# One layer with delta-rule heads, latent attention and experts: the output norm of a head pair apart from its scan, and another order of the opening

## The chip, the cores and the metric

The kernel runs on one core of a Trainium2 chip. Its time is the time of one execution on the device in microseconds (us); several executions are timed and the median is given. A profiled execution is a further one, with its own time.

## The reference

A stream `x` of 512 tokens and a context `ctx` of 256 tokens, 1024 channels each, go through one layer. What matters here is its first half:

```python
mod = silu(cond) @ ada_w + ada_b            # six vectors: shift, scale, gate, twice
h   = rms_norm(x) * g * (1 + scale) + shift # x by c, ctx by c_ctx
p   = h @ w_in                              # q, k, v, z of 8 heads, alpha, beta, and more
q, k, v = silu(short_conv(...))             # five taps over the tokens
o   = gated_delta_chunked(...)              # per head, forwards and backwards: ctx first
y   = rms_norm(o, dn_norm_g) * silu(z)      # the output norm of a head
```

After that come latent attention over the 768 tokens, the merge of both branches, and sixteen experts with 320 slots in all by expert choice.

## The kernel before, in words

**Layout.** Tokens stand in tiles of 128. `XT` holds the normed tokens transposed, eight tiles of 128 channels by 768 tokens (512 of `x`, then 256 of `ctx`). `HT` holds the modulated `x`, `HC` the modulated `ctx`; each value and each weight is split into a high and a low part, and a product is three matmuls (`begin`, and `mm3` at L140 to L142): high by high, high by low, low by high. The low part of a weight is `raw - high`.

**The opening, 0 to some 75 us.** `modulate(i)`, i = 0 to 3, makes 256 channels of the modulation. `aq{i}` (2 MB of `ada_w`, in two halves) is loaded, TensorE multiplies it (`pa{i}`), ScalarE copies the product (`ms{i}`), TensorE turns it into columns (`pc{i}`), VectorE makes shift and scale (`md`, `gs1`), ScalarE writes the high part of two tiles of `HT` (`ht`) and of `HC` (`hc`), and the low part is a product (`hm`) and a subtraction. `begin(i, name)` starts the projection of the first head's k, q and v (`wf0`, `wf1`, `wf2`) and of the second head's k (`wf3`) over those two tiles, six matmuls for each. `tokens(k)` and `tokens_ctx(k)` transpose one tile of channels of `x` and of `ctx`. All of it is written in one fixed order: `TE`, `SE`, `VE` and `GP` are wrappers (`_Pinned`) that keep each engine's instructions in the order of the program. All the large loads are issued on SyncE's queue, one after the other; an issue that waits for its buffer holds up the ones behind it.

**The head pairs, 75 to some 700 us.** For four pairs p of heads: `head_k`, `head_q`, `head_v`, `head_z` project, convolve and norm (`load_split` makes the low part `wl_*` of a weight on VectorE, L338); `prepare(p)` makes the decay matrices (TensorE `GH`, `gr`, ScalarE `D` with a Relu and an exponential, L759 and L760, VectorE `W` and `A`); `inverse(p)` inverts them, a long loop on VectorE; `scan(p)` walks over six steps of tokens in both directions. At its end `scan` norms the pair's output `O`: eight squares with a row sum on ScalarE (L996), four small operations on GpSimd (L997 to L1000), a product on VectorE (L1001), then eight transposes `py` on TensorE (L1009) and a product with the gate `Z`.

**The order of the pairs.** Each of these is a generator that `_Emit` steps: a job has a rank, a list of jobs that must be done before it (`after`), and each `yield` gives a cost and a latency on a planned clock. The job of lowest rank that is ready is written next, and the framework's scheduler orders what follows from that. `scan(p)` waits for `inverse(p)`, `prepare(p)` for the heads of p and for `dn[p - 1]`, which is the scan before, its norm and its `py` included; the heads of pair p wait for `dn[p - 2]`. Between the pairs stand jobs that fill TensorE: the projections for the gates (`gt`, `wl_gt`) and the latent attention, and `ada(q)`, the other modulation vectors (loads `aw`, matmuls `pa` at L168 and L170).

Of the kernel before, what the change touches and what calls it, by code (L numbers as in the profile page):

```python
# [20 lines left out]
P = 128  # L21
# [153 lines left out]
def hybrid_block(ctx: ExitStack, tc: tile.TileContext, I, out, dbg=None):  # L175
# [79 lines left out]
    for t in range(6):  # L255
        xt = vw.tile([P, D], F32, name=f"xt{t}")
        src = I["x"][0, t * P:(t + 1) * P, :] if t < 4 else I["ctx"][0, (t - 4) * P:(t - 3) * P, :]
        nc.sync.dma_start(xt, src)
        xn.append(xt)
# [112 lines left out]
    def split_first(j):  # L372
# [7 lines left out]
        first[nm] = (w, pdn([P, 512], f"pl_{nm}"))  # L380
# [30 lines left out]
    def modulate(i):  # L411
# [6 lines left out]
        m = vw.tile([P, 512], F32, tag="ms", name=f"ms{i}", bufs=2)  # L418
        SE.activation(m, pa, AF.Copy)
        yield  # L420
        pc = ptr([P, 4, P], f"pc{i}")
        for k in range(4):
            TE.transpose(pc[:, k], m[:, k * P:(k + 1) * P], ident)
# [8 lines left out]
        yield  # L432
        for sl, j in SEG:
            if j:
                yield
            for kk in range(2):
                k, h = 2 * i + kk, (HC if j else HT)[i][:, kk]
                if j == 0:
                    ys[kk] = vw.tile([P, TOK], F32, tag=f"xt{kk}", name=f"hm{k}")
                y = ys[kk]  # L440
                SE.activation(h[:, 0], XT[:, k, sl], AF.Identity, bias=md[:, i, 0, kk, j:j + 1],
                              scale=gs1[:, i, kk, j:j + 1])
                VE.tensor_scalar(y[:, sl], XT[:, k, sl], gs1[:, i, kk, j:j + 1], md[:, i, 0, kk, j:j + 1],
                                 op0=OP.mult, op1=OP.add)
                (GP if j else VE).tensor_sub(h[:, 1], y[:, sl], h[:, 0].bitcast(F32))
        yield

    ys = {}

    def begin(i, *names):  # L450
        for nm in names:
            w, pl = first[nm]
# [18 lines left out]
    m = [modulate(i) for i in range(NB)]  # L471
# [3 lines left out]
    tokens(0)  # L475
    norm(4)
    tokens(1)
    norm(5)
    for k in range(2, KT):
        tokens(k)  # L480
    for k in range(2):
        tokens_ctx(k)
    next(m[0])
    split_first(0)
    next(m[0])
    next(m[0])
    split_first(1)
    split_first(2)
    next(m[1])
    next(m[1])  # L490
    begin(0, "k0", "q0")
    next(m[1])
    begin(0, "v0")
    begin(1, "k0", "q0", "v0")
    for k in range(2, KT):
        tokens_ctx(k)
    next(m[0])
    split_first(3)
    next(m[2])
    next(m[2])  # L500
    begin(0, "k1")
    next(m[2])
    next(m[1])
    begin(2, "k0", "q0")
    next(m[3])
    begin(2, "v0")
    next(m[3])
    begin(1, "k1")
    next(m[3])
    next(m[2])  # L510
# [401 lines left out]
    def scan(p, zjobs):  # L912
# [9 lines left out]
        for s in range(6):  # L922
# [68 lines left out]
            yield 0.9, 0.5, None  # L991
        tap(f"O{p}", O)
# [21 lines left out]
    seq, A_jobs, zj, dn, dp_, dd = [], {}, {}, {}, {}, {}  # L1014
# [53 lines left out]
    dn[3] = em.add(3, scan(3, zj[3]), after=[dp_[3], dn[2]])  # L1068
# [744 lines left out]
```

## Time and profile before

| | |
|---|---|
| Median of 3 runs | 1776.95 us (1773.66 to 1779.38) |
| The profiled execution | 1781.53 us, its span 1779.8 us |
| TensorE (PE) busy | 1597.0 us, 90% of the span |
| VectorE (DVE) busy | 877.9 us, 49% |
| ScalarE (ACT) busy | 593.2 us, 33% |
| GpSimd (POOL) busy | 249.8 us, 14% |
| Mean granted clock of TensorE | 0.956 of full speed |

PE is the matrix engine, PEld its loading of weights, SPq SyncE's queue of DMA issues. A row of a timeline has the start, the duration, the engine, the line, the operation, the output and its inputs, and in brackets how long the engine was idle before it and what ended that. A granted clock of 1.00 is 2.4 GHz, of 0.50 it is 1.2 GHz.

### The profile page before, as it was taken

To read this page: it belongs to the slowest core of one execution; us is meant where nothing else is said; L and a number is where in the kernel's file an instruction comes from. 1 tells how busy PE (TensorE), PEld (TensorE's weight loads), DVE (VectorE), ACT (ScalarE), POOL (GpSimd) and SP (SyncE) were. 2 spreads that over 40 slices of the span, in tenths; PEclk is the share of its full clock that TensorE was granted. 3 is DMA by queue.
4 is the path that set the end of the run, shared out by engine and by line. 5 is a ranking of instruction groups with operands and counts; after the bars stand their busy time and mean duration, and the time that the engine had idled before them with its cause. 6 is when DMAs were issued, how large, how long until landed. Compare 5 with 4: busy or idle time off the path is not lost.

```text
span 1779.8 us, 25305 instructions
## 1 busy us (share of the span) xinstructions
PE 1597.0 (90%) x9990; PEld 1102.4 (62%) x9990; DVE 877.9 (49%) x1957; ACT 593.2 (33%) x1336; POOL 249.8 (14%) x326
## 2 busy tenths in 40 slices
PE   5897999898799997889989996999999999999887
PEld 4686887786678786767777775544454444444333
DVE  3687857965787854666873436121212121213122
ACT  4576338326634334556663423100010000000000
POOL 2222021121121122323121432000000000000000
PEclk8998999999899989899989997999999999999999
DMA  9211311343122342121126965799999999999997
GB/s 309 59 48 48 90 43 48 85 159 103 48 72 76 91 132 81 53 85 42 35 67 204 288 209 203 272 413 413 413 397 413 413 413 412 414 414 413 414 413 290
DMA packets 168409, 382.31 MB, mean 215 GB/s; under 512 B 10373, under 2 KB 91491, under 8 KB 168291
## 3 DMA queue, kind: packets, MB, share of 16 engines
q1 hardware_dynamic: 163328, 372.98, 56.6%
q10 hardware_dynamic: 4963, 7.72, 1.3%
q8 instruction: 78, 1.28, 0.3%
q14 instruction: 40, 0.33, 0.1%
HBM read 366.51 MB, written 14.16 MB: 214 GB/s over the span
## 4 chain that ended last, share of the span: by engine, by line
PE 40%; DMA 9%; DVE 5%; ACT 2%; issue 2%; POOL 2%; SPq 0%; DVEq 0%; ACTq 0%; POOLq 0%
PE pd L1765 7%; PE pg L1724 6%; PE pu L1724 5%; DMA wd<-in_w_down_dram 4%; PE pg L1725 3%; PE pu L1725 3%; PE pc L1781 2%; DMA w_up<-in_w_up_dram 1%; PE pxe L1667 1%; DMA woraw<-in_w_o_dram 1%; PE pxe L1668 1%; PE pPT L1311 1%; DMA raw_ukv<-in_w_ukv_dram 1%; PE px L140 1%; PE px L142 1%
## 5 line engine op out<-in xcount | busy, mean ns | idle before, releaser
L1724 PE MATMUL pg<-w_gate,XE 128*64 128x320 f32 x496 | 178.6, 511 | 0.0
L1724 PE MATMUL pu<-w_up,XE 128*64 128x320 f32 x480 | 160.0, 487 | 3.9 <-DMA w_up<-in_w_up_dram 3.9
L1745 DVE TENSOR_TENSOR hd<-hd,pu 128x320 f32<-128x320 f32 (+1 forms) x48 | 18.6, 416 | 287.7 <-PE pu L1725 270.5
L1725 PE MATMUL pg<-w_gate,XE 128*64 128x320 f32 x496 | 157.1, 455 | 0.0
L1765 PE MATMUL pd<-wd,hd 128*64 128x512 f32 x668 | 150.6, 597 | 3.1 <-DMA wd<-in_w_down_dram 3.1
L1725 PE MATMUL pu<-w_up,XE 128*64 128x320 f32 x480 | 153.3, 444 | 0.0
L1770 ACT ACTIVATE yo<-hd 128x512 fp32r<-128x512 f32 x16 | 10.1, 629 | 344.0 <-DVE hd L1769 344.0
L1724 PEld LDWEIGHTS pu<-w_up,XE 128*64 128x64 f32 x480 | 64.6, 137 | 74.3 <-issue 38.1
L1765 PEld LDWEIGHTS pd<-wd,hd 128*64 128x64 f32 x668 | 45.0, 136 | 86.4 <-issue 76.7
L1724 PEld LDWEIGHTS pg<-w_gate,XE 128*64 128x64 f32 x496 | 66.7, 141 | 45.7 <-issue 26.0
L1725 PEld LDWEIGHTS pg<-w_gate,XE 128*64 128x64 f32 x496 | 60.4, 140 | 23.7 <-issue 10.2
L1743 ACT ACTIVATE hd<-pg 128x320 f32<-128x320 f32 (+1 forms) x48 | 16.5, 378 | 171.5 <-PE pg L1725 171.5
L1781 PE MATMUL pc<-yo 64*128 64x512 f32 x256 | 47.3, 455 | 26.1 <-ACT yo L1770 22.7
L1781 PEld LDWEIGHTS pc<-yo 64*128 64x128 f32 x256 | 23.2, 194 | 66.7 <-ACT yo L1770 35.9
L1785 DVE TENSOR_TENSOR xm<-xm,pc 128x512 f32<-128x512 f32 x72 | 45.9, 683 | 32.0 <-PE pc L1781 32.0
L1769 DVE SCALAR_TENSOR_TENSOR hd<-pd,gs,m 128x512 f32<-128x512 f32 x16 | 12.0, 751 | 97.6 <-PE pd L1765 97.6
L142 PE MATMUL pl_gt<-ht,wl_gt 128*128 128x512 f32 x128 | 51.5, 402 | 3.1 <-DVE wl_gt L338 3.1
L1671 ACT ACTIVATE XE<-pxe,mod,gs 128x256 f32<-128x256 f32 x32 | 16.3, 560 | 112.6 <-PE pxe L1668 99.9
L140 PE MATMUL pl_gt<-ht,wh_gt 128*128 128x512 f32 x128 | 53.2, 416 | 0.0
L1725 PEld LDWEIGHTS pu<-w_up,XE 128*64 128x64 f32 x480 | 49.8, 135 | 2.8
L141 PE MATMUL pl_gt<-ht,wh_gt 128*128 128x512 f32 x128 | 51.3, 400 | 0.0
L1160 DVE TENSOR_TENSOR PT<-pPT,PT 128x512 fp32r<-128x512 f32 x48 | 33.0, 688 | 24.9 <-ACT PT L1159 24.7
(623 smaller groups left out, 4214.8 us busy)
## 6 DMA issues: line engine op xcount, KB each, us to landing
w_gate<-in_w_gate_dram SPq DMA_DIRECT2D x60, 1408.0 KB, 14.9
w_up<-in_w_up_dram SPq DMA_DIRECT2D x60, 1408.0 KB, 19.8
wd<-in_w_down_dram SPq DMA_DIRECT2D x45, 1536.0 KB
aw<-in_ada_w_dram SPq DMA_DIRECT2D x32, 512.0 KB, 5.7
wd<-in_w_down_dram SPq DMA_DIRECT2D x15, 1024.0 KB, 15.9
aq<-in_ada_w_dram SPq DMA_DIRECT2D x8, 1024.0 KB, 9.2
raw_gt<-in_w_in_dram SPq DMA_DIRECT2D x16, 512.0 KB, 3.8
ring_w<-in_w_up_dram SPq DMA_DIRECT2D x3, 1408.0 KB, 12.6
```

Of the source, the lines that this page charges most:

```text
L140: nc.tensor.matmul(out, wh, xh, start=first, stop=False)
L141: nc.tensor.matmul(out, wh, xl, start=False, stop=False)
L142: nc.tensor.matmul(out, wl, xh, start=False, stop=last)
L1160: nc.vector.tensor_sub(lo, src, hi.bitcast(F32))
L1311: nc.tensor.transpose(p_[:, t * P:(t + 1) * P], Pm[:, t, kt_ * P:(kt_ + 1) * P], ident)
L1667: nc.tensor.matmul(px[:, j], X2[:, t, 0, ks], oh, start=(t == 0), stop=False)
L1724: nc.tensor.matmul(dst[c][0:64, :n], x_, w[kk][:, o:o + n], start=(k == ko[0]), stop=(k == ko[3] + 1))
L1725: nc.tensor.matmul(dst[c][64:128, :320], x_, w[kk][:, FA + c * 320:FA + c * 320 + 320], start=(k == ko[0]), stop=(k == ko[3] + 1))
L1745: nc.vector.tensor_mul(hd[pr, o:o + b - a], hd[pr, o:o + b - a], pu[c][pr, a:b])
L1765: nc.tensor.matmul(pd[64 * dh:64 * dh + 64], l_, w[:, j, dh * 512:(dh + 1) * 512], start=(i == 0), stop=(i == 10))
L1781: nc.tensor.matmul(pcs[dh], o_[ps_, t, :], y_[ps_, l, :], start=(i + l == 0), stop=(i + l == len(ys_)))
L1785: nc.vector.tensor_add(xm[t][:, sl], xm[t][:, sl], pcs[dh])
```

## The change

It has three parts.

1. **Loads and order of the opening.** The two loads of `ctx` come after the weights of the modulation and of the first heads; they go into a buffer of the tag `aq`. The first half of `aq0`, then `k0`, then its second half come first. `modulate(i)` is taken apart into `ada_block(i)`, `columns(i)` and `modulate(i, j)`, j = 0 for `x` and 1 for `ctx`; all `modulate(i, 1)` stand at the end.
2. **Engines.** The four low parts of `wf` (128 by 1024) and the eight low parts of `HC` (128 by 256) are subtracted on VectorE and not on GpSimd.
3. **The norm apart.** `scan(p)` ends with its last step (`sc[p]`), and `finish(p)` (`dn[p]`, rank p + 0.5) holds the norm and `py`. Heads of pair p wait for `sc[p - 2]`, `prepare(p)` for `sc[p - 1]`; `scan(p)` waits for `dn[p - 1]`.

```diff
-    for t in range(6):
+    for t in range(4):
         xt = vw.tile([P, D], F32, name=f"xt{t}")
-        src = I["x"][0, t * P:(t + 1) * P, :] if t < 4 else I["ctx"][0, (t - 4) * P:(t - 3) * P, :]
...
+    def load_ctx():
+        a = vr.tile([P, 2, KT, 2 * P], F32, tag="aq", name="xctx", bufs=3).rearrange("p l k c -> p (l k c)")
+        for t in range(2):
+            xn.append(a[:, t * D:(t + 1) * D])
+            nc.sync.dma_start(xn[4 + t], I["ctx"][0, t * P:(t + 1) * P, :])
...
-        GP.tensor_sub(w[1], raws[j], w[0].bitcast(F32))
...
+    def split_lo(j):
+        w = first[FIRST[j][0]][0]
+        VE.tensor_sub(w[1], raws[j], w[0].bitcast(F32))
...
-                (GP if j else VE).tensor_sub(h[:, 1], y[:, sl], h[:, 0].bitcast(F32))
...
+    def modulate(i, j):
+        sl = SEG[j][0]
+        for kk in range(2):
...
+            VE.tensor_scalar(y, XT[:, k, sl], gs1[:, i, kk, j:j + 1], md[:, i, 0, kk, j:j + 1],
+                             op0=OP.mult, op1=OP.add)
+            VE.tensor_sub(h[:, 1], y, h[:, 0].bitcast(F32))
...
+    begin(3, "k0")
+    norm(4)
+    norm(5)
+    begin(3, "q0", "v0")
+    for k in range(4):
         tokens_ctx(k)
...
+    begin(0, "k1")
+    begin(1, "k1")
+    for k in range(4, KT):
         tokens_ctx(k)
...
+    for i in range(NB):
+        modulate(i, 1)
     begin(2, "k1")
+    begin(3, "k1")
...
+        DN[p] = O
+
+    def finish(p, zjobs):
+        O = DN[p]
         tap(f"O{p}", O)
...
-            add_heads(p, after=[dn[p - 2]] if p > 1 else ())
-        prev = [dn[p - 1]] if p else []
+            add_heads(p, after=[sc[p - 2]] if p > 1 else ())
+        prev = [sc[p - 1]] if p else []
...
-            dn[p] = em.add(p, scan(p, zj[p]), after=[dp_[p]])
+            sc[p] = em.add(p, scan(p), after=[dp_[p]] + ([dn[p - 1]] if p else []))
+            dn[p] = em.add(p + 0.5, finish(p, zj[p]), after=[sc[p]])
```

**SyncE's queue in the opening.** The issues of the kernel before, then of the change (`raw_k0` is the first head's k weight, `raw_k1` the second head's):

```order
L258 DMA xt4_121<-in_ctx_dram 128x1024
L258 DMA xt5_123<-in_ctx_dram 128x1024
L363 DMA aq0_145<-in_ada_w_dram 128x8x256 x2
L369 DMA raw_k0_148<-in_w_in_dram 128x8x128
L369 DMA raw_q0_150<-in_w_in_dram 128x8x128
L363 DMA aq1_152<-in_ada_w_dram 128x8x256 x2
L369 DMA raw_v0_155<-in_w_in_dram 128x8x128
L363 DMA aq2_157<-in_ada_w_dram 128x8x256 x2
L369 DMA raw_k1_160<-in_w_in_dram 128x8x128
L363 DMA aq3_162<-in_ada_w_dram 128x8x256 x2
L465 DMA abw_104<-in_w_in_dram 128x8x32
```

```order
L363 DMA aq0_141<-in_ada_w_dram 128x8x256
L374 DMA raw_k0_143<-in_w_in_dram 128x8x128
L363 DMA aq0_141<-in_ada_w_dram 128x8x256
L374 DMA raw_q0_146<-in_w_in_dram 128x8x128
L363 DMA aq1_148<-in_ada_w_dram 128x8x256 x2
L374 DMA raw_v0_151<-in_w_in_dram 128x8x128
L363 DMA aq2_153<-in_ada_w_dram 128x8x256 x2
L363 DMA aq3_156<-in_ada_w_dram 128x8x256 x2
L374 DMA raw_k1_159<-in_w_in_dram 128x8x128
L369 DMA xctx_161<-in_ctx_dram 128x1024 x2
L475 DMA abw_104<-in_w_in_dram 128x8x32
```

The two loads of `ctx` moved from ahead of `aq0` to behind `raw_k1`, and `aq3` from behind `raw_k1` to ahead of it.

**TensorE just behind the opening,** at some 75 to 90 us: `pl_q1` is the second head's q projection (24 matmuls of 128 by 512; its third one needs `wl_q1`, a low part that VectorE makes), `pl_ab` that of alpha and beta (24 matmuls), `ptn` are transposes of the first head's convolved q and k. Before, then now:

```order
L140 MATMUL pl_q1_689<-ht0_139,wh_q1_684 128x512
L141 MATMUL pl_q1_689<-ht0_139,wh_q1_684 128x512
L635 MATMUL ptn_q00_672<-cst0_81,qv0_581 128x128 x4
L140 MATMUL pl_ab_750<-ht0_139,abh_562 96x512
...
L142 MATMUL pl_ab_750<-ht0_139,abl_563 96x512
L635 MATMUL ptn_k00_696<-cst0_81,qk0_580 128x128 x4
L142 MATMUL pl_q1_689<-ht0_139,wl_q1_685 128x512
```

```order
L140 MATMUL pl_q1_698<-ht0_135,wh_q1_693 128x512
L141 MATMUL pl_q1_698<-ht0_135,wh_q1_693 128x512
L140 MATMUL pl_ab_759<-ht0_135,abh_571 96x512
...
L142 MATMUL pl_ab_759<-ht1_136,abl_572 96x512
L649 MATMUL ptn_k00_705<-cst0_81,qk0_589 128x128 x4
L764 MATMUL GH04_1080<-qk0_589 128x128
L649 MATMUL ptn_q00_681<-cst0_81,qv0_590 128x128 x4
L649 MATMUL ptn_k04_715<-cst0_81,qk0_589 128x128 x2
L142 MATMUL pl_q1_698<-ht0_135,wl_q1_694 128x512
```

Between the left-out lines stand 9 matmuls of `pl_ab` in all before, and all 24 now; the other 15 stood behind `pl_q1` before.

**ScalarE at the norm of pair 0,** at some 260 us: `ro0<-O0` are the squares, `D14` and `D15` two decay matrices of `prepare(1)`, `cx_k4` copies of a projection. Before, then now:

```order
L996 ACTIVATE junk_579,ro0_2543<-O0_2230 128x128 x6
...
L996 ACTIVATE junk_579,ro0_2543<-O0_2230 128x128 x2
...
L759 ACTIVATE D14_2585<-gr14_2584,gg_574 128x128 x4
...
L760 ACTIVATE D14_2585<-D14_2585 128x512
L759 ACTIVATE D15_2625<-gr15_2624,gg_574 128x128 x4
```

```order
L1014 ACTIVATE junk_588,ro0_2552<-O0_2239 128x128
L773 ACTIVATE D14_2580<-gr14_2579,gg_583 128x128
...
L774 ACT_TABLE_LOAD
L774 ACTIVATE D14_2580<-D14_2580 128x512
L1014 ACTIVATE junk_588,ro0_2552<-O0_2239 128x128
L773 ACTIVATE D15_2620<-gr15_2619,gg_583 128x128
```

The decay matrices of the next pair now alternate with the squares, and a table load and an exponential stand between the fifth and the sixth square. On TensorE the matmuls behind them (`GH14`, `gr14`, `GH15`, `gr15`, twelve in all) moved from behind `py` of pair 0 to ahead of it.

## Rows read from the trace of the kernel before

**Rows 1.** View by stretches, first 40 us (columns: us, busy us of each engine, PEclk, DMA share, GB/s).

```profile
0.00:40.00 40.00, 19.89 (x128) 14.20 (x129) 16.51 (x29) 18.29 (x30) 12.96 (x19) 0.87 0.97 304
```

**Rows 2.** Timeline from 22.9 to 30 us (start, us, engine, line, operation, out<-in).

```profile
24.70 2.34 POOL L153 TENSOR_TENSOR wf<-raw_k,wf 128x1024 fp32r<-128x1024 f32 x1 [5.88 <-ACT wf L153]
...
27.07 0.37 SPq L369 DMA_DIRECT2D raw_v<-in_w_in_dram  x1
```

**Rows 3.** View by stretches, TensorE alone (us, busy us, PEclk, DMA share, GB/s).

```profile
26.59:36.83 10.24, 6.61 (x41) 0.50 1.01 309
```

**Rows 4.** Waits of TensorE, 0 to 80 us (total us, times, longest us).

```profile
PE pa L153 <- DMA aq<-in_ada_w_dram: 3.7, 2, 2.8
```

**Rows 5.** Groups by shape, 0 to 80 us (count, busy us, mean ns, idle before).

```profile
L153 PE MATMUL pcx<-cst,xt 128*128 128x128 f32 x16 | 2.6, 287 | 0.5 <-ACT XT L153 0.5
...
L153 DVE TENSOR_TENSOR ht<-hm,ht 128x512 fp32r<-128x512 f32 x8 | 5.5, 692 | 1.5 <-ACT ht L153 1.1
...
L153 ACT ACTIVATE hc<-XT,md,gs 128x256 fp32r<-128x256 f32 x8 | 4.2, 587 | 0.0
```

**Rows 6.** Timeline of TensorE, 60 to 94 us.

```profile
60.59 4.72 PE L153 MATMUL pl_k<-ht,wf 128*128 128x512 f32 x18
...
69.34 0.28 PE L140 MATMUL pc_k<-hc,wf 128*128 128x256 f32 x1
...
75.03 0.40 PE L140 MATMUL pl_q<-ht,wh_q 128*128 128x512 f32 x1
...
80.97 0.50 PE L142 MATMUL pl_q<-ht,wl_q 128*128 128x512 f32 x1
...
93.64 0.29 PE L140 MATMUL pc_k<-hc,wf 128*128 128x256 f32 x1
```

**Rows 7.** Timeline of VectorE, 66 to 81 us.

```profile
66.64 0.96 DVE L623 TENSOR_SCALAR qk<-cx_k,CW 128x512 f32<-128x512 f32 x1
...
68.67 0.95 DVE L519 TENSOR_TENSOR abl<-abw,abh 128x768 fp32r<-128x768 f32 x1
...
79.70 1.21 DVE L338 TENSOR_TENSOR wl_q<-raw_q,wh_q 128x1024 fp32r<-128x1024 f32 x1
```

**Rows 8.** Timeline at the norm of pair 0, 260 to 269 us.

```profile
260.23 0.31 ACT L996 ACTIVATE junk<-O 128x128 bf16<-128x128 f32 x1 [2.35 <-POOL O L990]
...
263.82 0.19 ACT L996 ACTIVATION_READ_ACCUMULATOR junk<-O 128x1 f32 x1
...
268.55 0.79 PE L1009 MATMUL py<-cst,O 128*128 128x128 f32 x4 [3.31 <-DVE O L1001]
```

**Rows 9.** Timeline of ScalarE, 119 to 126 us.

```profile
119.72 1.13 ACT L759 ACTIVATE D<-gr,gg 128x128 f32<-128x128 f32 x4
120.89 0.63 ACT L760 ACTIVATE D<-D 128x512 f32<-128x512 f32 x1
123.88 1.28 ACT L628 ACT_TABLE_LOAD   x1 [2.36 <-DVE qk L626]
125.18 0.85 ACT L628 ACTIVATE qk<-qk 128x768 f32<-128x768 f32 x1
```

**Rows 10.** Timeline of TensorE at the norm of pair 1.

```profile
409.14 1.06 PE L168 MATMUL pa<-aw,cl 128*32 128x512 f32 x1 [4.65 <-DMA aw<-in_ada_w_dram]
...
413.71 1.09 PE L1009 MATMUL py<-cst,O 128*128 128x128 f32 x8 [0.51 <-DVE O L1001]
```

**Rows 11.** View by stretches of 10 us (busy us of each engine).

```profile
410.00:420.00 10.00, 9.47 (x65) 6.48 (x58) 4.43 (x8) 6.39 (x14) 2.78 (x5) 0.89 0.51 154
...
470.00:480.00 10.00, 8.46 (x26) 6.59 (x27) 9.32 (x20) 1.26 (x2) 0.00 (x0) 0.66 0.41 106
```

**Rows 12.** Waits of TensorE, 80 to 450 and 450 to 712 us.

```profile
PE pD L771 <- POOL D L761: 1.7, 1, 1.7
...
PE ptn_k L635 <- ACT qk L628: 5.3, 1, 5.3
...
PE pl_gt L142 <- DVE wl_gt L338: 3.1, 1, 3.1
```

More of the change, by code (lines that the diff above doesn't have):

```diff
@@ L417, in modulate, with columns @@
                               aq[i][:, l, k0 + g], start=(k0 == 0), stop=(k0 == 4))
[L418 to L420 removed]
+        ms[i] = vw.tile([P, 512], F32, tag="ms", name=f"ms{i}", bufs=2)
+        SE.activation(ms[i], pa, AF.Copy)
+    def columns(i):
         pc = ptr([P, 4, P], f"pc{i}")
         for k in range(4):
[L423 removed]
+            TE.transpose(pc[:, k], ms[i][:, k * P:(k + 1) * P], ident)
         VE.tensor_reduce(md[:, i].rearrange("p l k j -> p (l k) j"),
@@ L431, in modulate @@
                                 op0=OP.add, op1=OP.mult)
[L432 to L444, printed above, removed]
-                (GP if j else VE).tensor_sub(h[:, 1], y[:, sl], h[:, 0].bitcast(F32))
-        yield
-    ys = {}
+    def modulate(i, j):
+        sl = SEG[j][0]
+        for kk in range(2):
+            k, h = 2 * i + kk, (HC if j else HT)[i][:, kk]
+            y = vw.tile([P, SEQ], F32, tag=f"xt{kk}", name=f"hm{k}{j}")[:, :sl.stop - sl.start]
+            SE.activation(h[:, 0], XT[:, k, sl], AF.Identity, bias=md[:, i, 0, kk, j:j + 1],
+                          scale=gs1[:, i, kk, j:j + 1])
+            VE.tensor_scalar(y, XT[:, k, sl], gs1[:, i, kk, j:j + 1], md[:, i, 0, kk, j:j + 1],
+                             op0=OP.mult, op1=OP.add)
+            VE.tensor_sub(h[:, 1], y, h[:, 0].bitcast(F32))
+    ms = {}
     def begin(i, *names):
         for nm in names:
+            if i == 0:
+                first[nm][1] = pdn([P, 512], f"pl_{nm}")
             w, pl = first[nm]
@@ L474, in hybrid_block @@
     vectors()
-    tokens(0)
+    for k in range(4):
+        tokens(k)
+    split_hi(0)
+    split_lo(0)
+    for k in range(4, KT):
+        tokens(k)
+    ada_block(0)
+    split_hi(1)
+    columns(0)
+    modulate(0, 0)
+    split_lo(1)
+    begin(0, "k0", "q0")
+    ada_block(1)
+    split_hi(2)
+    columns(1)
+    modulate(1, 0)
+    begin(1, "k0", "q0")
+    ada_block(2)
+    split_lo(2)
+    begin(0, "v0")
+    columns(2)
+    modulate(2, 0)
+    begin(1, "v0")
+    ada_block(3)
+    begin(2, "k0")
+    columns(3)
+    modulate(3, 0)
+    begin(2, "q0", "v0")
+    split_hi(3)
+    split_lo(3)
+    begin(3, "k0")
     norm(4)
-    tokens(1)
     norm(5)
-    for k in range(2, KT):
-        tokens(k)
-    for k in range(2):
+    begin(3, "q0", "v0")
+    for k in range(4):
         tokens_ctx(k)
[L483 to L495, printed above, removed]
-        tokens_ctx(k)
[L497 to L510, printed above, removed]
+    begin(0, "k1")
+    begin(1, "k1")
+    for k in range(4, KT):
+        tokens_ctx(k)
+    for i in range(NB):
+        modulate(i, 1)
     begin(2, "k1")
-    begin(3, "k0", "q0", "v0", "k1")
-    next(m[3])
+    begin(3, "k1")
     vr_close()
@@ L910, in inverse, with scan @@
             yield 0, 2, None
-    def scan(p, zjobs):
+    def scan(p):
         qk, qv = QK[p], QV[p]
@@ L1067, in hybrid_block @@
     dp_[3] = em.add(PRM["r3"], inverse(3), after=[dd[3], dp_[2]])
-    dn[3] = em.add(3, scan(3, zj[3]), after=[dp_[3], dn[2]])
+    sc[3] = em.add(3, scan(3), after=[dp_[3], dn[2]])
+    dn[3] = em.add(3.5, finish(3, zj[3]), after=[sc[3], dn[2]])
     em.until(dn[2], *fills, dp_[3])
```

32 lines of the change are left out of this document (17 added, 15 removed).

## The prediction, made before the change was run

> **What bounds the kernel now.** I read the page first (TensorE busy 90% of the span), then TensorE's waits by stretch, then the timelines where the change cuts. The busy share is not the limit of the places that change. In the first 40 us TensorE is busy 19.89 us, its granted clock is 0.87, and the DMA engines are at a share of 0.97 with 304 GB/s [rows 1]: the loads set the pace. It waits 3.7 us for halves of `aq`, once 2.8 [rows 4], and behind that stands a stretch of 10.24 us at clock 0.50, the lower level of 1.2 GHz, with 6.61 us of work [rows 3]. GpSimd's low part of 2.34 us from 24.70 holds SyncE's queue: the load of `raw_v` is issued at 27.07, just behind its end [rows 2]. Behind the opening, from 66.64 us, VectorE convolves the first head and makes `wl_q`, which ends at 79.70 + 1.21 = 80.91, and TensorE goes on with `pl_q` at 80.97 [rows 7, 6]: there VectorE is the limit. At the pairs the reader should see short waits, each for another engine: 3.31 us for the normed output of pair 0 [rows 8], 4.65 for a load of `aw` and 0.51 for pair 1's output [rows 10], 5.3 for a silu of k [rows 12].
>
> **The opening.** Everything up to and with `aq3` is now loaded before `raw_k1` and `ctx`: constants 0.07 MB, `x` 2.1, four blocks 8.4, three weights 1.6, together 12.2 MB, at 304 GB/s [rows 1] 40 us; with the landing I take 42. From there TensorE has work in hand: half of the last block and its columns, about 2.5 us, then ten groups of six matmuls. The six groups from 60.59 to 69.34 took 8.75 us [rows 6], 1.46 each, so ten take 14.6. The context's transposes take 2.6 and wait 0.5 for copies [rows 5]. Sum: 42 + 2.5 + 14.6 + 3.1 = 62.2, against 69.34 before. The last context copy lies two groups (2.9 us) ahead of this, at some 60; ScalarE's eight parts `hc` then take 4.2 us [rows 5] and end at about 65, since they stand behind all copies.
>
> The low parts are VectorE's now. The four of `wf` cost what `wl_q` does, 1.21 [rows 7]; the eight of `HC` half of `ht`'s 0.692 [rows 5], 0.35. Together 7.6 us. The first four lie where VectorE waits for blocks; without that cover they cost up to 4.8 us. The eight alternate with `hc` (4.2 for ScalarE against 8 x 0.35 plus their products): VectorE follows closely and ends at 65.6. In return SyncE's queue no longer waits for GpSimd.
>
> So `pc_k` ends at about 66, `pc_v` needs half of 75.03 - 69.34 = 5.7 us [rows 6], and `pl_q` begins at 68.9: 6.1 us earlier than 75.03. Not all of it is kept. VectorE begins the convolution at 65.6, only 1.0 before 66.64 [rows 7]. Between that and `wl_q`, `abl` goes (0.9 [rows 7]), and two short sums of some 0.4 come in: `wl_q` ends at 79.8, 1.1 us earlier. TensorE has in front of it two matmuls of `pl_q`, all 24 of `pl_ab` and ten transposes, 26 x 0.24 + 1.2 = 7.4, so it stands there at 76.3 and waits 3.5 us. But then it has done 15 matmuls of `pl_ab` (3.6 us) and two transposes (0.2) that it did behind 80.97 before. Its lead at `pc_k` of the second head, 93.64 before [rows 6], is 1.1 + 3.8 = 4.9.
>
> That wait of 3.5 us is new, and the row for such a wait is [rows 3]: behind 2.8 us the clock was 0.50 and 6.61 us of work took twice as long, 3.3 us lost. I take half, 1.7, as some of what follows waits anyway. **The opening is worth -3.2 us** (ends: -1.0, if only VectorE's earlier start passes on, and -6.1, if all does).
>
> **The norm at pairs 0 and 1.** Before, the squares ran from 260.23 to 264.01, and `py` began 4.5 us after their end [rows 8]. Now seven Relu of 1.13/4 [rows 9], 2.0 us, an exponential of 0.63 and a table load of 1.28 [rows 9] stand among them: 3.9 us later, `py` at 272.4. In return twelve matmuls that stood behind `py` are done before it; by `py`'s own four in 0.79 [rows 8] they are worth 2.4 us. Net +1.5. At pair 1 twenty such matmuls move ahead, most into the wait of 4.65 for `aw` [rows 10], 20 x 1.09/8 = 2.7 us; `py` is again 3.9 later, net +1.2. Behind `py` on TensorE are the next projections, so the delay is paid there and not hidden.
>
> What the delay buys: `prepare(1)` has its decay matrices some 3 us earlier, so TensorE's wait of 1.7 us for `D` [rows 12] goes: -1.7. Late next is `py` itself. Together **+1.0** (ends: -3 and +4).
>
> By the Trainium skill, "ScalarE: Activation LUTs", section "What ACT_TABLE_LOAD costs", each switch of the function set costs about 2.66 us, 1.28 for the load and 1.38 for a drain, and functions should be batched by set. Here a load of 1.28 at 123.88 is followed by the next activation at 125.18 [rows 9], 0.02 us behind it: the trace shows the load and no drain behind it.
>
> **Pairs 2 and 3.** The change lets `prepare(2)` and the loop of `inverse(2)` begin some 4 us earlier. VectorE has room there, 4.43 of 10 us busy at 410 to 420, and none later, 9.32 at 470 to 480 [rows 11], where TensorE waits 5.3 us for a silu behind a convolution [rows 12]. Work pulled into the idle stretch shortens that wait; no row shows by how much. Bounds 0 and 5.3; I take **-3**, a little under the 4 us by which the work moves. From 690 us on, the order of TensorE is the same as before, and the experts wait for nothing that changes: what is won there stays.
>
> **Sum.** -3.2 + 1.0 - 3.0 = -5.2 us. Against the profiled execution 1781.5 - 5.2 = 1776.3; the median of the runs lies 4.6 lower, so 1776.95 - 5.2 = **1771.7 us**. About 0.3%, 5.3 us, is what a measurement of this kernel can tell from no change; the forecast stands on that bound.
>
> **The rivals.**
> - *The opening's lead is swallowed.* VectorE is full from 66.64 to `wl_q` [rows 7], so for it speaks that only its own 1.0 us counts; against it, that 15 `pl_ab` fill the wait. With nothing won at pairs 2 and 3: -1.0 + 1.0 = 0, 1777.
> - *The waits behind 440 us go.* The lead of 6.1 with the lost clock of 1.7 off, -4.4, pairs 0 and 1 at +1.0, the wait of 5.3 wholly gone and with it a loss of clock of 3.3 as in [rows 3]: -12.0, 1765. For it the idle VectorE in [rows 11], against it that other waits come up.
> - *Slower: the splits of pair 3 come late.* In VectorE's new order `wl_k6` stands 27 places further back, behind the work of `prepare(2)`, and `pl_k6` on TensorE is queued behind it, with all projections of heads 6 and 7. A wait of this kind is 3.1 us for `wl_gt` [rows 12], with 3.3 of lost clock 6.4. Three splits (k, q, v) can be hit; it decides when two are, 12.8 against -3.2 + 1.0: +10.6, 1787.5. Against it speaks the free time at 410 to 420.
> - *The drain.* By a drain of the table as long as the load (1.28) `py` would be 1.3 us later at each of three norms: -5.2 + 3.9 = -1.3, 1775.7. The rows speak against it. The page named above would make it 1.38.
>
> **Chances.** Forecast 0.48 (its own range 1766 to 1777), swallowed 0.17, waits gone 0.14, slower 0.18, drain 0.03. Faster by over 0.3%: 0.30 of the forecast, for its centre lies on the bound and a gain behind 440 us is likelier than a loss, and 0.14: 0.44, with the edge of the second case 0.45. Slower: 0.18 and 0.02 of the swallowed case: 0.20. The rest, 0.35, is no change. The range goes from 1758, which holds the greater part of the gain with its unknown size, to 1785, which holds one late split (-2.2 + 6.4, 1781) and half of the case with two.
>
> **What would show it.** Right: `pl_q` of the second head starts near 69 us and waits some 3.5 us for `wl_q`, and `pc_k` of the second head begins near 89 (with a clock of 0.50 near 91). `py` of pair 0 begins about 4 us later relative to the last step of the scan, pD's wait is gone, and the wait for the silu of k near 466 is shorter. Wrong: TensorE's lead at 95 us is under 2 us; or waits for `wl_k`, `wl_q` or `wl_v` appear at 420 to 470 us; or the lead at 690 us differs from the lead at the end.

## The result, and the profile after

The change runs in 1788.51 us (median of 18, 1783.29 to 1796.44), the kernel before, on the same chip, in 1779.47 (median of 18, 1773.66 to 1784.31). The ratio is 1.0052, 95% interval 1.004 to 1.0063: **slower by 0.5%**. The forecast was 1771.7, and the time lies above the upper end of its range, 1785.

| | before | change |
|---|---|---|
| Profiled execution, its span | 1781.53, 1779.8 us | 1783.35, 1781.6 us |
| TensorE busy | 1597.0 us | 1593.9 us |
| VectorE, ScalarE, GpSimd busy | 877.9, 593.2, 249.8 us | 874.5, 585.1, 231.3 us |
| Mean granted clock | 0.956 | 0.964 |

The change's profiled execution is one of its fastest, 5.2 us under its median, and that of before 2.1 above its own, so the two traces show less of the loss than the medians do. A second profile of the unaltered change (1787.66 us) stands beside it below. The profile of the opening alone is the slowest of its executions (1787.81, median 1784.07), so its last rows show more than its median.

The busy times hardly tell anything. I therefore followed the end of the same matmuls through both traces. Each entry is the end of the last matmul of a tile, less its end in the trace of before (negative is earlier):

| | before, us | change | change again | opening alone | norm alone |
|---|---|---|---|---|---|
| `pl_v` of head 0 | 68.1 | -10.1 | -10.7 | -11.2 | 0.4 |
| `pc_ab` | 93.8 | -0.3 | -0.9 | -1.5 | 0.4 |
| second `pl_ckv` | 231.8 | 2.9 | 2.0 | 1.6 | -0.8 |
| fourth `pl_z` | 373.1 | 4.0 | 3.1 | 3.0 | -1.1 |
| `py` of pair 1 | 414.8 | 8.4 | 7.0 | 3.2 | 3.2 |
| `pl_v` of head 6 | 444.0 | 20.1 | 20.4 | 3.2 | 17.3 |
| last `pl_gt` | 606.8 | 3.7 | 5.5 | 3.5 | 0.6 |
| `pq` of the attention | 698.0 | 1.0 | 3.9 | 4.3 | 1.1 |
| last matmul of the experts | 1768.5 | 1.8 | 6.2 | 6.3 | -0.3 |

Two things are seen: a lead of 10 us at 68 us that is gone at 94, and a hole of 12 us behind pair 1 that is later filled up again. The first is smaller than it looks. Before, three of the four `pl_k` groups of the second head and all context transposes stood ahead of this `pl_v`; now they stand behind it. At the first `pc_k`, which has the same work ahead of it in both kernels, the lead is 2.6 us (66.70 against 69.34 [rows 6]).

**The opening.** The first 40 us of the change, as in [rows 1] (columns: us, busy us of PE, PEld, DVE, ACT, POOL, PEclk, DMA share, GB/s):

```profile
0.00:40.00 40.00, 21.63 (x128) 14.36 (x129) 15.63 (x28) 15.57 (x24) 4.04 (x12) 0.89 1.01 316
```

Two stretches of it for TensorE alone, as in [rows 3] (us, busy us, PEclk, DMA share, GB/s):

```profile
24.67:31.50 6.83, 6.57 (x24) 0.50 1.13 335
38.33:41.74 3.41, 3.41 (x12) 0.50 1.11 340
```

The DMA engines moved 316 GB/s instead of 304, and no wait for `aq` is left where before there were 3.7 us [rows 4]. But the clock of 0.50, the lower level, lasts 10.24 us in two stretches, as long as before [rows 3], and TensorE is busy for 9.98 of them (6.61 before). Its timeline against [rows 5, 6]:

```profile
27.61 2.76 PE L153 MATMUL pl_q<-ht,wf 128*128 128x512 f32 x6
...
46.80 1.93 PE L153 MATMUL pa<-aq,cl 128*32 128x256 f32 x32
...
50.51 1.65 PE L153 MATMUL pl_q<-ht,wf 128*128 128x512 f32 x6
...
63.82 3.04 PE L153 MATMUL pl_k<-ht,wf 128*128 128x512 f32 x12
66.70 0.28 PE L140 MATMUL pc_k<-hc,wf 128*128 128x256 f32 x1
...
84.62 0.50 PE L142 MATMUL pl_q<-ht,wl_q 128*128 128x512 f32 x1 [0.76 <-DVE wl_q L337]
...
93.33 0.29 PE L140 MATMUL pc_k<-hc,wf 128*128 128x256 f32 x1
```

A group of six costs 2.76 us at 27.61 and 1.65 at 50.51. TensorE comes to the last block at 46.80 and finds it loaded. ScalarE next:

```profile
57.06 1.28 ACT L585 ACT_TABLE_LOAD   x1
58.35 0.22 ACT L585 ACTIVATE alv<-alv 128x16 f32<-128x16 f32 x1
...
64.38 4.04 ACT L153 ACTIVATE hc<-XT,md,gs 128x256 fp32r<-128x256 f32 x8
```

And VectorE, against [rows 7]:

```profile
65.00 0.43 DVE L153 TENSOR_TENSOR hc<-hm,hc 128x256 fp32r<-128x256 f32 x1 [5.26 <-ACT hc L153]
65.35 0.41 DVE L153 TENSOR_SCALAR hm<-XT,gs,md 128x256 f32<-128x256 f32 x1
65.86 0.42 DVE L153 TENSOR_TENSOR hc<-hm,hc 128x256 fp32r<-128x256 f32 x1
...
71.33 0.48 DVE L637 TENSOR_SCALAR qk<-cx_k,CW 128x512 f32<-128x512 f32 x1
...
83.34 1.22 DVE L337 TENSOR_TENSOR wl_q<-raw_q,wh_q 128x1024 fp32r<-128x1024 f32 x1
```

VectorE stands idle for 5.26 us, then needs 0.86 us for each pair of `hm` and `hc` (65.00 to 65.86), and begins the convolution at 71.33: 4.7 us **later** than before (66.64). `wl_q` is 3.6 later (79.70 before). TensorE begins `pl_q` of the second head at 73.88, 1.2 us earlier than before, and then stands still for 2.7 us in three waits before 84.62, the last of them for `wl_q`. With that its lead is used up.

**Pair 1.** ScalarE in the change (before, the squares stood together: 3.4 us from 406.09):

```profile
410.72 0.31 ACT L1014 ACTIVATE junk<-O 128x128 bf16<-128x128 f32 x1 [4.00 <-POOL O L1004]
...
411.02 0.35 ACT L773 ACTIVATE D<-gr,gg 128x128 f32<-128x128 f32 x1
...
413.32 1.28 ACT L774 ACT_TABLE_LOAD   x1
414.61 0.63 ACT L774 ACTIVATE D<-D 128x512 f32<-128x512 f32 x1
...
416.23 0.30 ACT L1014 ACTIVATE junk<-O 128x128 bf16<-128x128 f32 x1
...
435.58 6.25 ACT L817 ACTIVATE inv<-W 32x768 f32<-32x768 f32 x4
441.86 0.60 ACT L635 ACTIVATE cx_k<-pl_k 128x512 f32<-128x512 f32 x1
```

TensorE at both norms, against [rows 8, 10], and at the projection behind:

```profile
273.61 1.78 PE L1027 MATMUL py<-cst,O 128*128 128x128 f32 x8 [2.58 <-DVE O L1019]
...
421.21 1.97 PE L1027 MATMUL py<-cst,O 128*128 128x128 f32 x8 [2.49 <-DVE O L1019]
...
442.50 0.50 PE L140 MATMUL pl_q<-ht,wh_q 128*128 128x512 f32 x1 [3.28 <-ACT cx_k L635]
```

The eight squares now take 5.9 us, with Relu, a table load and an exponential of pair 2 among them. What matters more stands further down. Four copies of the diagonal blocks of `W` into `inv` (L817, the head of `inverse(2)`) hold ScalarE for 6.25 us, and `cx_k`, the copy that empties `pl_k` of head 6, comes behind them. TensorE's waits in the change, 404 to 500 us (total, times, longest), and behind them VectorE's row for `inv`:

```profile
PE pl_q L140 <- ACT cx_k L635: 3.3, 1, 3.3
...
PE GH L764 <- ACT D L773: 2.7, 2, 2.2
PE py L1027 <- DVE O L1019: 2.5, 1, 2.5
```

```profile
DVE inv L818 <- ACT inv L817: 5.7, 1, 5.7
```

### The profile page after: what moved, and what is told of

Its sections match the earlier page's. It is cut to its first block, busy times and chain, and to the rows that moved or that the text cites. A ratio compares the mean times of both kernels' runs of the same rounds, so it can differ in the third digit from the quotient of the medians.

```text
span 1781.6 us, 25312 instructions
## 1 busy us (share of the span) xinstructions
PE 1593.9 (89%) x9990; PEld 1098.2 (62%) x9990; DVE 874.5 (49%) x1969; ACT 585.1 (33%) x1332; POOL 231.3 (13%) x314
## 4 chain that ended last, share of the span: by engine, by line
PE 40%; DMA 10%; DVE 5%; ACT 2%; issue 2%; POOL 1%; SPq 0%; DVEq 0%; ACTq 0%; POOLq 0%
PE pd L1785 7%; DMA wd<-in_w_down_dram 5%; PE pg L1744 5%; PE pu L1744 5%; PE pg L1745 3%; DMA w_up<-in_w_up_dram 3%; PE pu L1745 2%; PE pc L1801 2%; PE pxe L1687 1%; PE pxe L1688 1%; PE px L140 1%; DMA raw_ukv<-in_w_ukv_dram 1%; PE px L141 1%; PE px L142 1%; PE pPT L1331 1%
## 5 line engine op out<-in xcount | busy, mean ns | idle before, releaser
L1744 PE MATMUL pg<-w_gate,XE 128*64 128x320 f32 x496 | 174.9, 502 | 1.1 <-DMA w_gate<-in_w_gate_dram 1.1
L1745 PE MATMUL pg<-w_gate,XE 128*64 128x320 f32 x496 | 153.4, 448 | 0.0
L1790 ACT ACTIVATE yo<-hd 128x512 fp32r<-128x512 f32 x16 | 10.1, 630 | 345.0 <-DVE hd L1789 345.0
```

The lines of the kernel that those rows point to most:

```text
L1744: nc.tensor.matmul(dst[c][0:64, :n], x_, w[kk][:, o:o + n], start=(k == ko[0]), stop=(k == ko[3] + 1))
L1745: nc.tensor.matmul(dst[c][64:128, :320], x_, w[kk][:, FA + c * 320:FA + c * 320 + 320], start=(k == ko[0]), stop=(k == ko[3] + 1))
```

## The experiments

Each kernel was timed in five rounds beside the kernel before on its chip (1777.4 to 1779.5 us there).

### The parts alone

`opening only` leaves the norm inside `scan`; `norm only` keeps the old opening.

> The change's opening alone (loads, block by block, low parts on VectorE); the output norm stays inside the scan. From the second head pair on, TensorE's order is that of the kernel before. Theory A (the opening gives its lead back, since VectorE begins the first convolution at 71.33 us instead of 66.64, and the norm apart makes the loss): within 3 us of before, TensorE at pc_ab of the second head level within 1 us. Theory B (the opening makes the loss): +6 to +10 us. My forecast for this term was -3.2.

> The norm apart alone, with the opening of before; from pair 0's scan on TensorE's order is that of the change. Theory A: the whole loss, +6 to +10 us, with py of pair 0 some 5 us and py of pair 1 some 7 us later than before relative to the scans. Theory B: within 3 us of before. My forecast for this part was -2.0.

Measured: the opening alone 1784.07, ratio 1.0024 (1.0014 to 1.0035), slower; the norm alone 1780.13, ratio 1.0000 (0.9988 to 1.0013). The change once more, unaltered:

> The change once more, unaltered, beside the next three on one chip, since its profiled execution stands only 1.8 us above that of before while its median stands 9.0 above. Theory C (the loss is +4.3 for the opening and the rest for the norm, and the first profile was a fortunate execution): ratio 1.003 to 1.006 again, and this profile shows more than +3 us at the end. Rival (part of the 9.0 came from the chip it ran on): ratio under 1.003.

1788.92, ratio 1.006 (1.0038 to 1.0081). So the loss is real and the opening alone has about half of it. In the traces the two parts add up (at 607 us 3.5 and 0.6, against 3.7 and 5.5 in the two traces of the change); in the medians 4 to 5 us of the change's loss are in neither part alone, and these traces don't show where. The norm alone shows the hole of the change at 444 us almost whole (17.3), with the same order on ScalarE, and yet loses nothing at the end:

```profile
431.44 6.27 ACT L803 ACTIVATE inv<-W 32x768 f32<-32x768 f32 x4
437.74 0.60 ACT L621 ACTIVATE cx_k<-pl_k 128x512 f32<-128x512 f32 x1
```

### The opening: where VectorE begins

The first edit puts the context modulation of the first two blocks ahead of the second half of the transposes, in the change and in the opening alone:

```diff
     for k in range(4):
         tokens_ctx(k)
+    for i in range(2):
+        modulate(i, 1)
     begin(0, "k1")
     begin(1, "k1")
     for k in range(4, KT):
         tokens_ctx(k)
-    for i in range(NB):
+    for i in range(2, NB):
         modulate(i, 1)
```

> The change, with the context modulation of blocks 0 and 1 ahead of the second half of the context transposes, and only blocks 2 and 3 at the end. VectorE then has four pairs of product and subtraction (0.86 us each) less in front of the first convolution: it begins near 68 us instead of 71.33. Theory A on the opening (VectorE's chain carries the time there): 2 to 4 us faster than the change. Rival (TensorE's lead is lost further on, whatever VectorE does): within 1 us of the change.

> The new opening alone, with the context modulation in two halves, and the norm inside the scan. Theory (VectorE's late start costs the opening its lead): 3 to 5 us faster than the new opening alone, level with before or up to 3 us faster. Rival (the gain of the halves in the change was an interplay with the norm): within 1.5 us of the new opening alone, some 4 us slower than before.

Measured: 1783.93, ratio 1.0018 (0.9999 to 1.0037), with the norm apart, and 1782.46, 1.0020 (1.0006 to 1.0035), without. VectorE's convolution begins at 64.61 and 67.42 instead of 71.33 and 70.20, and the lead at `pc_ab` is 6.3 and 1.9 us. Against their kernels without the edit that is 4.6 us, where I had said 2 to 4, and 1.6, where I had said 3 to 5. VectorE's start moves as meant; what it brings at the end is small here. The second edit tried to free VectorE in another way, with the low parts of `HC` on GpSimd again, in the opening alone:

```diff
-            VE.tensor_sub(h[:, 1], y, h[:, 0].bitcast(F32))
+            (GP if j else VE).tensor_sub(h[:, 1], y, h[:, 0].bitcast(F32))
```

> The new opening alone, with the eight low parts of the context back on GpSimd (0.8 us each there, 0.43 here); all else as in the new opening alone. Theory A (VectorE's start of the first convolution sets the time behind the opening): it starts some 2.5 to 3.5 us earlier, and the kernel is 2 to 4 us faster than the new opening alone. Rival (the context's low parts come later and TensorE's pc_k waits for GpSimd as long as it did for VectorE): within 1.5 us of the new opening alone.

1782.23, ratio 1.0029 (1.0015 to 1.0043). This test misses its object. The two buffers `hm` come free only when GpSimd has subtracted, so VectorE waits for them and begins the convolution at 71.06 (70.20 in the opening alone). GpSimd's timeline, then VectorE's, in this kernel:

```profile
67.44 1.48 POOL L153 TENSOR_TENSOR hc<-hm,hc 128x256 fp32r<-128x256 f32 x2 [0.29 <-DVE hm L153]
```

```profile
70.01 1.13 DVE L153 TENSOR_SCALAR hm<-XT,gs,md 128x256 f32<-128x256 f32 x2 [0.62 <-POOL hc L153]
71.06 0.95 DVE L637 TENSOR_SCALAR qk<-cx_k,CW 128x512 f32<-128x512 f32 x1
```

### ScalarE's order at the norm

`SE` is the wrapper that keeps the order of the program. The edit gives it the eight squares of every norm, and the Relu and exponential of every decay:

```diff
-                nc.scalar.activation(Dm[:, m], gr[:, m], AF.Relu, bias=gg[:, t, col(m):col(m) + 1], scale=-1.0)
-            nc.scalar.activation(Dm, Dm, AF.Exp, scale=-1.0)
+                SE.activation(Dm[:, m], gr[:, m], AF.Relu, bias=gg[:, t, col(m):col(m) + 1], scale=-1.0)
+            SE.activation(Dm, Dm, AF.Exp, scale=-1.0)
...
-                nc.scalar.activation(junk[:, 0:P], O[:, t, a], AF.Square, accum_out=r[:, t, a:a + 1])
+                SE.activation(junk[:, 0:P], O[:, t, a], AF.Square, accum_out=r[:, t, a:a + 1])
```

First in the change, then with the edit of the opening too, then with the old opening, then in the kernel before with neither part.

> The change, with ScalarE held to the order of the program for the eight squares of a norm and for the decay matrices, so that no Relu, table load or exponential stands between the squares. Theory A: py of pairs 0 and 1 comes some 4 us earlier than in the change, and at least half of the loss goes: 4 to 9 us faster than the change. Rival (the loss comes from other waits that the new order makes behind 415 us, not from the squares): within 2 us of the change.

> The change with both mends: context modulation in two halves, and ScalarE held to program order for squares and decay matrices. Theory (the two act in different places and add up): 2 to 5 us faster than with the norm first alone, 6 to 10 us faster than before. Rival (the waits behind 415 us swallow what the opening brings): like the norm first alone, 4 to 5 us faster than before.

> The opening of before, the norm apart and ScalarE held to program order; from pair 0's heads on TensorE's order is that of the norm first. Theory (the opening costs 4 us wherever it stands): 3 to 5 us faster than the norm first with the new opening, 7 to 10 us faster than before. Rival (the opening's shift decides how the later waits fall): within 2 us of the norm first with the new opening.

> The kernel before with nothing but ScalarE held to program order for the squares of a norm and the decay matrices. Before, the squares stand together anyway. Theory A (what the hold mends is the interleaving that the norm apart made): within 2 us of before, so that the norm apart together with the hold is what wins the 4 us. Rival (the hold itself helps the decay matrices, with or without the norm apart): 3 to 6 us faster than before.

Measured, in this order: 1774.83, ratio 0.9969 (0.9956 to 0.9983); 1772.65, 0.9973 (0.9956 to 0.9989); 1774.67, 0.9972 (0.9958 to 0.9986); **1771.31, 0.9958 (0.994 to 0.9976)**. With the norm apart and the order held, neither the halves of the opening nor the old opening brings anything over the unaltered one, where I had expected 2 to 5 us. The last run fells the theory that I went in with, that the held order only repairs what the norm apart does: it is worth 0.4% in the kernel before, where no decay matrix stands among the squares. What it changes there is further on. ScalarE in the kernel before:

```profile
444.17 1.62 ACT L803 ACTIVATE inv<-W 32x768 f32<-32x768 f32 x1
446.72 1.59 ACT L803 ACTIVATE inv<-W 32x768 f32<-32x768 f32 x1
449.11 2.98 ACT L803 ACTIVATE inv<-W 32x768 f32<-32x768 f32 x2
452.51 0.58 ACT L621 ACTIVATE cx_v<-pl_v 128x512 f32<-128x512 f32 x1
```

and in the kernel before with the held order:

```profile
443.73 0.60 ACT L621 ACTIVATE cx_v<-pl_v 128x512 f32<-128x512 f32 x1
444.23 1.64 ACT L803 ACTIVATE inv<-W 32x768 f32<-32x768 f32 x1
447.83 4.92 ACT L803 ACTIVATE inv<-W 32x768 f32<-32x768 f32 x3
```

`cx_v` moves ahead of the copies into `inv`, and TensorE's wait for it goes, which the trace of before lists from 404 to 500 us as

```profile
PE pl_k L140 <- ACT cx_v L621: 3.7, 1, 3.7
```

So the same copies hold up TensorE in the kernel before already; whether that is the 0.4% is tested below. Next, the order was held in the change at one place only, the squares of pair 1 and the decay of pair 2:

```diff
-                nc.scalar.activation(Dm[:, m], gr[:, m], AF.Relu, bias=gg[:, t, col(m):col(m) + 1], scale=-1.0)
-            nc.scalar.activation(Dm, Dm, AF.Exp, scale=-1.0)
+                (SE if p == 2 else nc.scalar).activation(Dm[:, m], gr[:, m], AF.Relu, bias=gg[:, t, col(m):col(m) + 1], scale=-1.0)
+            (SE if p == 2 else nc.scalar).activation(Dm, Dm, AF.Exp, scale=-1.0)
...
-                nc.scalar.activation(junk[:, 0:P], O[:, t, a], AF.Square, accum_out=r[:, t, a:a + 1])
+                (SE if p == 1 else nc.scalar).activation(junk[:, 0:P], O[:, t, a], AF.Square, accum_out=r[:, t, a:a + 1])
```

> The change with ScalarE held to program order at one place only: the norm of pair 1 with the decay matrices of pair 2; all else up to 415 us is as in the change. Theory A (the loss sits at pair 1 and the waits behind it at 415 to 460 us): 8 to 14 us faster than the change, near the kernel with all norms first. Rival (pair 0 and the rest carry half of it): 3 to 7 us faster than the change.

1778.33, ratio 0.9994 (0.998 to 1.0008): 10 us of the change come back at this one place. Its ScalarE:

```profile
410.90 0.31 ACT L153 ACTIVATE junk<-O 128x128 bf16<-128x128 f32 x1 [4.00 <-POOL O L1004]
...
413.94 0.31 ACT L153 ACTIVATE junk<-O 128x128 bf16<-128x128 f32 x1
...
434.43 0.60 ACT L635 ACTIVATE cx_k<-pl_k 128x512 f32<-128x512 f32 x1 [0.55 <-PE pl_k L142]
434.92 6.61 ACT L817 ACTIVATE inv<-W 32x768 f32<-32x768 f32 x4
```

Two things differ here: the squares stand together, and `cx_k` stands ahead of the copies.

### The copies of the diagonal blocks

To tell these two apart, the copies of pair 2 were given to VectorE, which is idle for 5.7 us there, and the squares left as they are in the change:

```diff
-            nc.scalar.activation(Dg[q, :, 0:24].rearrange("p i m -> p m i"), W[q, :, q], AF.Copy)
+            if p == 2:
+                nc.vector.tensor_copy(Dg[q, :, 0:24].rearrange("p i m -> p m i"), W[q, :, q])
+            else:
+                nc.scalar.activation(Dg[q, :, 0:24].rearrange("p i m -> p m i"), W[q, :, q], AF.Copy)
```

> The change with one thing: the four copies of W's diagonal blocks into inv of pair 2 are made by VectorE instead of ScalarE; squares and decay are left interleaved as in the change. In the change these copies hold ScalarE for 6.25 us from 435.58, the projection's copy cx_k of head 6 stands behind them, TensorE waits 3.28 us for it at half the clock after, and VectorE is idle for 5.65 us for inv. Theory G (of the 10 us that the held order at pair 1 gave back, most is cx_k's place behind these copies): TensorE's wait of 3.28 goes, the lead of 20 us lost at the projection of v of head 6 shrinks to 12 or less, and the time falls by 4 to 9, to 1780 to 1785. Theory H (the interleaved squares themselves, py 3 us later and what follows, are the loss; what stands behind comes late anyway): 1787 to 1790 as the change.

1776.73, ratio 0.9987 (0.9972 to 1.0002): **12 us under the change, with the squares still interleaved**, more than its whole loss of 9, where I had expected 4 to 9. So the loss at pair 1 hangs on the place of `cx_k` and the time of the copies, and it goes although the squares are left as they are. (Some projections behind this place change their order too.) The timelines of VectorE, ScalarE and TensorE in this kernel:

```profile
435.00 3.53 DVE L818 COPY inv<-W 32x768 f32<-32x768 f32 x4
```

```profile
435.52 0.60 ACT L635 ACTIVATE cx_k<-pl_k 128x512 f32<-128x512 f32 x1 [1.01 <-PE pl_k L142]
```

```profile
437.94 0.40 PE L140 MATMUL pl_q<-ht,wh_q 128*128 128x512 f32 x1
```

`cx_k` is copied 6.3 us earlier, TensorE's wait of 3.3 us is gone, and `inv` is ready at 438.5 instead of 441.8. But `pl_v` of head 6 still ends 14.4 us later than in the kernel before, where I had said 12 or less: the greater part of the hole in the first table is no loss at the end. The same edit in the kernel before tells whether this repairs the change or is a gain of its own:

> The kernel before with the same one thing as the last run: the four copies of pair 2's diagonal blocks made by VectorE. It tells whether those 12 us were a repair of the change or a gain of its own. In the kernel before, too, a projection's copy (cx_v of head 6, 452.51) stands behind these copies on ScalarE (from 444.17), TensorE waits 3.7 us for it and VectorE 7.30 us for inv. Theory I (one mechanism, present before the change already; the held order helped the kernel before by the same way): 1769 to 1773, 6 to 10 below before. Theory J (only the change puts a head in the way; before, the copies alternate with its work): 1776 to 1781, as before.

1777.81, ratio 0.9993 (0.9982 to 1.0004): no gain. The wait for `cx_v` does go and TensorE is 4.2 us ahead at `pl_k` of head 7, but at the ninth `pl_gt` (546 us) it is 0.2 behind: TensorE now waits 3.3 us for `E` of the inversion, where `wl_gt` was late before [rows 12].

```profile
PE gr L757 <- DVE E L873: 3.3, 1, 3.3
```

Behind this wait the granted clock is 0.50 from 515.8 to 536.3 us, with TensorE busy throughout; in the kernel before it is 0.50 from 514.7 to 521.5. TensorE alone from 400 to 560 us in the kernel before, in the kernel before with the held order, and in this one (us, busy us, PEclk, DMA share, GB/s):

```profile
400.00:560.00 160.00, 137.43 (x1040) 0.93 0.26 74
```

```profile
400.00:560.00 160.00, 139.26 (x1092) 0.97 0.27 78
```

```profile
400.00:560.00 160.00, 142.03 (x1042) 0.87 0.25 74
```

The means over all executions go the same way: a clock of 0.958 for the kernel before on these chips, 0.964 with the held order and 0.956 here, 0.959 for the change and 0.962 with its copies on VectorE. So a part of these gains and losses is the clock behind the waits, and no run here separates it from the waits themselves. Nor is it shown why the held order gains 0.4% in the kernel before: the wait for `cx_v` alone, which this kernel is rid of too, is not enough. The same freed time is worth 12 us in one order and nothing in the other.

### The three parts together

`e12` is the change with the held order and `modulate(i, 1)` directly behind `tokens_ctx(2i)` and `tokens_ctx(2i + 1)`, for each block; `e15` is the same kernel again, `e13` the same with the norm inside `scan`, `e14` the unaltered opening with the held order and the norm inside, `e18` is `e13` with the copies of pair 2 on VectorE.

> As with both mends, and the context modulation of each block directly behind its own two transposes, so that only one block stands in front of the first convolution on VectorE instead of two. Theory A on the opening: VectorE begins 1.5 to 2 us earlier and the kernel is 1 to 2 us faster than with both mends. Rival (ScalarE, which now alternates copies and high parts, holds up the transposes): within 1 us of both mends or slower.

> The kernel before with two things: the new opening with each block's context modulation directly behind its own two transposes, and the eight squares of each norm and the decay's Relu and exponential held in program order on ScalarE; the norm stays in the scan. Theory C: once the order on ScalarE is held, the norm apart only moves py's work and ScalarE's heads to worse places and costs some 3 us (with the old opening 1774.7 against 1771.3), so without it this kernel beats both mends with quarters (1768.4) by about 3: 1765, from 1763 to 1767. Theory D: the norm apart is worth nothing either way once the order is held, and the difference of 3.4 us came from where in the order its jobs fell with the old opening: this kernel then stands within 1.5 us of 1768.4, 1767 to 1770. Theory E: the norm apart is what lets the opening's lead through pair 1 (without it the next projections of pair 2 cannot start before the norm): this kernel is then slower than 1770.

> The change's opening, unaltered, with the norm inside the scan and the order of squares, Relu and exponential held on ScalarE: the last corner of the three parts (opening, norm apart, held order). The opening alone cost 4.3 us without the held order. Theory C (each part costs what it costs, the held order saves 8): before with the held order 1771.3 plus 4 = 1775.5, from 1774 to 1777. Theory F: the opening's loss, too, was an interleaving on ScalarE that the hold takes away: 1771, from 1769.5 to 1772.5, as with the norm apart the unaltered opening cost nothing under the hold (1774.8 against 1774.7).

> The change with the held order and each block's context modulation behind its own two transposes, run before, once more, for a comparison on one chip with the kernel whose norm stays in the scan. Every theory: 1768.4 within 1.5 us; the difference to the kernel without the norm apart is what counts.

> The new opening with each block's context modulation behind its own two transposes, the norm inside the scan, the order of squares, Relu and exponential held (1769.0), and the copies of pair 2's diagonal blocks on VectorE. If the held order and the copies' new engine mend one and the same wait (theory I), the two together give little more than one: 1765 to 1769. If they are two things, 8 us each: 1758 to 1762.

| ratio to before | norm in `scan` | norm apart |
|---|---|---|
| old opening | 1 | 1.0000 |
| new opening | 1.0024 | 1.0052 (again 1.006) |
| old opening, held order | 0.9958 | 0.9972 |
| new opening, held order | 0.9980 (0.9968 to 0.9993) | 0.9969 |
| opening block by block, held order | 0.9946 (0.9926 to 0.9966) | 0.9943 (0.9924 to 0.9962), again 0.994 (0.9922 to 0.9957) |

`e12` took 1768.39 us, `e13` 1768.98, `e14` 1774.57, `e15` 1768.46, and `e18` 1768.96 with a ratio of 0.9953 (0.9934 to 0.9972). With the order held and the opening mended, the norm apart makes no difference (`e13` against `e15`, on one chip). The held order and VectorE's copies don't add up: `e18` gains nothing over `e13`. That they mend one thing is not shown by it, for with the norm in the scan the copies on VectorE gave nothing without the held order either. The unaltered opening costs 0.2% with the order held as without it, if the norm is in the scan; with the norm apart that cost is not seen, which stays open. `e12` beats both kernels, by 0.6% and 1.1%. Its VectorE:

```profile
65.46 0.48 DVE L639 TENSOR_SCALAR qk<-cx_k,CW 128x512 f32<-128x512 f32 x1
...
77.87 1.22 DVE L337 TENSOR_TENSOR wl_q<-raw_q,wh_q 128x1024 fp32r<-128x1024 f32 x1
```

This is the start of 65.6 that I had forecast for the change, and with it the lead at `pc_ab` is 5.8 us, where I had put 4.9 at the `pc_k` behind it.

## Why the prediction was wrong

- **The opening, -3.2: it is about +4.** Three steps failed. *Loads set the pace*: "with the landing I take 42", then 2.5 us to the first of ten groups, 44.5. TensorE came to the last block at 46.80, without a wait for it, and to the groups at 48.66: its own work, 9.98 us of it at a clock of 0.50, was the limit, with 3.5 us of waits for `ht` of ScalarE (0.6 before). I had let the half clock of [rows 3] go with the waits for `aq`; the waits went, and the 10.24 us of it stayed. The ten groups and the transposes themselves took 18.2 us, near my 17.7. *"VectorE follows closely and ends at 65.6"*: the `hc` began at 64.38, and I had them done at 65; their 4.04 us fit. VectorE then needs 0.86 us a pair where I let a subtraction hide behind `hc`: it ended 2.9 us behind ScalarE, not 0.6. From there to the end of `wl_q` it was 13.2 us and not 14.2, which gave some back. So `wl_q` was ready at 84.56 and not 79.8, TensorE began `pl_q` at 73.88 and not 68.9, and the lead at `pc_k` of the second head was 0.3 us, not 4.9. The 1.7 us of lost clock that I put behind the new wait did not come: the clock is 1.00 from 80 to 105 us. Between 94 and 232 us 3 us more went; the opening mended block by block loses 2 there as well. From 100 to 116 us TensorE stands idle for 1.0 us in the change, in the opening alone and in the mended one, and not at all in the kernel before; the rest stays open.
- **The norm at pairs 0 and 1, +1.0.** From the first square to `py` it is 2.2 us longer at pair 0 (10.50 against 8.32) and 2.9 at pair 1, where I said 3.9 for each: sized too high. *"TensorE's wait for `D` goes"* failed: `pD` waits 5.8 us in four waits from 80 to 450 us, 1.7 before, and at pair 1 `GH` waits 2.7 us for ScalarE's `D`, a wait that I didn't have. And *"Late next is `py` itself"* is the step that hid the real cost. Late next was `cx_k`, 20 us further down ScalarE's queue.
- **Pairs 2 and 3, -3.** From `py` of pair 1 to the last `pl_gt` the change wins 4.7 us in one trace and 1.5 in the other, and the silu wait of 5.3 became 2.9 in two, with 2.2 for the silu of q beside them. The sum is near in the first trace; but the way is a loss of 12 us and a gain of 16. I looked at VectorE's idle time and not at what ScalarE does at the head of `inverse(2)`, the 6.25 us of copies that move earlier with it. Pulling a job forward pulls its bulk work in front of a short copy on another engine.
- **The rivals.** The one on the slower side gave 1787.5, close to the time, by a mechanism that did not happen: no wait for `wl_k`, `wl_q` or `wl_v` of heads 6 and 7 reaches a microsecond. Its class was right, a projection of head 6 held up by work of pair 2 in its way, on the wrong engine. The drain of a table load is not there: in the opening the next activation follows the load of 57.06 within 0.02 us, as in [rows 9]. The Trainium skill's 1.38 us of drain ("ScalarE: Activation LUTs", section "What ACT_TABLE_LOAD costs") is not seen in this trace either.
- **The chances.** Slower had 0.20. Two of the three terms rested on work that is moved on VectorE and ScalarE, and their ends were drawn around TensorE's rows. The lower end of the opening, -1.0, did not hold that VectorE could begin later than before.

## What to carry to other kernels

When a change lets a job start earlier, read the whole queue of each engine behind it, and look for a short copy that empties a PSUM tile (or a similar release) behind a bulk job: TensorE waits there although ScalarE is busy a third of the time. Where a scheduler makes the order, one edge moved reorders distant work; a held order at one place, or bulk copies on an engine that is idle there, shows whether a loss belongs to the change or to the order it fell into. Give the kernel before the same mend: only that tells a repair from a gain of its own. Compare the times of a tile in two traces where the same work stands ahead of it. A lead of TensorE is worth what the next engine in the chain can use of it, so work out that engine's start before the lead.

## What was not expected of the hardware

The same four copies of 32 by 768 elements, written in a permuted order (the two inner axes change places), took 6.25 us on ScalarE and 3.53 on VectorE. And a dependent pair on VectorE (a product of 128 by 256, then the subtraction that reads it) repeats every 0.86 us: the next product, which needs nothing from the subtraction, begins 0.35 us behind its start (65.00 to 65.35), the subtraction 0.51 behind the start of the product that it reads (65.35 to 65.86).
